# The output projection of 16 tiles in pairs, by seven products of quarters under one bounded scale

## The chip, the cores and the metric

The kernel runs on one core of one Trainium2 chip. Its time is the device time of one execution in microseconds (us); for a kernel the median of its runs is given. One execution was also recorded by the hardware profiler. The engines are called PE (TensorE matmul), PEld (its weight loads), DVE (VectorE), ACT (ScalarE), POOL (GpSimd) and SP (SyncE, which only issues DMAs here).

## What is computed

One step of a network layer for two groups of tokens: 2048 sample tokens and 128 prompt tokens, 2176 rows of 1024 float32 values. Three branches mix the tokens, each branch is projected to 1024 columns and gated, the three are added (`merged`), and one output projection, a residual add and a normalisation end it. The part that matters here:

```python
    br = jnp.stack([o_a, o_b, o_c], axis=2)
    pb = jnp.einsum('btnw,nwd->btnd', br, w_branch)
    gt = jax.nn.sigmoid(gates.reshape(B, T, N_BRANCH, D_MODEL))
    merged = jnp.einsum('btnd,btnd->btd', gt, pb)
    return jnp.einsum('btd,de->bte', merged, w_out), s_f, s_b
...
        out, _, _ = mixer(xn, *lp(l), state_delta[:, l, 0], state_delta[:, l, 1], (rows, GRID_W))
        h = h + gate[:, None, :] * out
    y_sample = rmsnorm(h, final_g)
```

`merged` is (2176, 1024), `w_out` is (1024, 1024). For the sample group the gate is one row of 1024 values, for the prompt group another.

## The kernel before

Rows are counted in 17 tiles of 128 (`P`): tiles 0 to 15 are the sample tokens, tile 16 the prompt. The 1024 columns of the model are eight blocks (`KT`) of 128. Every float32 operand of a large product is split into two float16 halves: it is multiplied by a power of two `s` found from its sum of squares (`scales`: a square with accumulated sum on ACT, a one-column matmul with ones on PE for the sum over the partitions, three integer steps on DVE), `hi` is the float16 of that (ACT), `lo` the float16 of the rest (DVE). A product then takes three matmuls per block of 128 in the contraction: hi·hi, hi·lo, lo·hi (`gemm_T`, `gemm_N`). A result is multiplied by the inverse scales where it leaves PSUM.

Three merges come one after the other, `merge(1)`, `merge(2)` and `merge(0)`, each adding one branch to `merged`, which is kept transposed in DRAM (`mD`: block of columns, 128, tokens). In a merge, for each column block `db` and each stretch of 512 tokens (the last stretch, the prompt, has 128): 24 matmuls of the gate from the normalised input `xh`, `xl` (which stays in SBUF all the time), a sigmoid on ACT, 12 matmuls of the branch projection from `o16` (in the pool `big`), the product on DVE (L1708), the addition to the old row on POOL (L1709), which SP has loaded (L1687); after each half of the tokens POOL's queue writes the row back (L1716). In the last merge `HALVES` is turned round, so tokens 1024 to 2175 come first in each block and tokens 0 to 1023 last. During it `out_w` loads and splits one block of `w_out` per `db`, and the gate rows are made. During the second merge the scan of the DeltaNet branch still runs, with its own loads in SP's queue.

After the last merge the output: tile 16, then tiles 8 to 15, then 0 to 7. For each tile `out_prep` loads the tile's eight blocks from `mD` (L1767), squares them, finds the scale and makes the halves (L1777 to L1780); this runs five tiles ahead of the products, for the first five already in the last merge. Then two products of 512 columns over eight blocks (48 matmuls a tile), the gate times the inverse scales on the way out of PSUM (L1841), the residual add on POOL (L1842), the square, the root and the scaling by `final_g` (L1860 to L1862) and the store. The last tile is cut into 512, 384 and 128 columns so that little is left after its last product.

The order on each engine is fixed when the program is built: a scheduler places the instructions by estimated durations and by priorities (`tc.high_priority`), and each engine then runs its list in order. SP's list holds nearly all loads and the stores of the results, so a load whose buffer is not free yet holds back all loads behind it. Buffers rotate within a pool by tag (`bufs`); memory of a closed pool is used again by later pools once its last readers are done. PSUM has eight banks: three in `ps_mm`, three in `ps_d`, two in `ps_x`.

Of the kernel before, what the change touches and what calls it, by code (L numbers as in the profile page):

```python
# [188 lines left out]
def hybrid_flow_kernel(ctx: ExitStack, tc: tile.TileContext, x_prompt, x_sample, state_delta, c, c_ctx, w_ada,  # L189
# [50 lines left out]
    def mm(out, l, r, start=True, stop=True):  # L240
        newest[0] = PE.matmul(out, l, r, start=start, stop=stop)  # L241
# [16 lines left out]
    def scales(ss, pl, tag, sb16=None):  # L258

        ps = bank(ps_x, [P, 1])  # L260
        mm(ps, ones16, widened(ss, pl, tag) if sb16 is None else sb16)
        t = sb(pl, [P, 4], tag)
        h = t[:, 3:4].bitcast(I32)
        V.tensor_scalar(h, ps.bitcast(I32), 24, None, ALU.logical_shift_right)
        V.tensor_scalar(t[:, 1:2].bitcast(I32), h, -8388608.0, 204.0 * 8388608, ALU.mult, ALU.add)
        V.tensor_scalar(t[:, 2:3].bitcast(I32), h, 8388608.0, 50.0 * 8388608, ALU.mult, ALU.add)
        return t[:, 1:2], t[:, 2:3]
# [20 lines left out]
    def converting(w, st, nkt, cols=P, hi=None, lo=None, tag="w", bufs=5):  # L288
# [9 lines left out]
        ss = sb(wp, [P, 1], "wss", bufs=4)  # L298
# [45 lines left out]
    for i, (n_, g) in enumerate(_blocks()):  # L344
        wlist.append((w_blk[i], KT, "z" if n_ == C_ZA else "v" if n_ == C_V else "w", 4))
        if n_ >= C_G:
            wlist.append((w_brb[(n_ - C_G) // D, g], 4, "b", 2))
# [4 lines left out]
    def read_next(p_=None):  # L352
# [4 lines left out]
        elif len(wread) < min(len(wdone) - len(wsteps) + 2, len(wlist)):  # L357
            src, nkt, tag, bufs = wlist[len(wread)]
            wread.append(read_w(src, nkt))

    def begin():
# [7 lines left out]
        wsteps.append(converting(wdone[i], wread[i], wlist[i][1], tag=wlist[i][2], bufs=wlist[i][3]))  # L369
# [1288 lines left out]
    def branch_scale(n, cols):  # L1658
        ss = sb(ep, [P, 1], "bss2")
        V.tensor_reduce(ss, oss[n][:, 0:cols], AX.X, ALU.add)  # L1660
        return scales(ss, ep, "bsc")
# [10 lines left out]
    def merge(n, first, inv, each=None, halves=HALVES, mid=None, then=None):  # L1672

        steps, sinv = iter(()), None
        for db in range(KT):
# [8 lines left out]
            for h0, hn, tbs in halves:  # L1684
# [5 lines left out]
                for t0, tn in tbs:  # L1690
                    if first and db == 0:
# [14 lines left out]
                    else:  # L1706
                        with tc.high_priority():
                            V.scalar_tensor_tensor(sg, ps, binv[:, 1:2], sg, ALU.mult, ALU.mult)  # L1708
                        G.tensor_tensor(mr, mr, sg, ALU.add)  # L1709
                    pace.tick(tn * MT)  # L1710
# [5 lines left out]
                (SY if first else G).dma_start(mD[db][:, h0:h0 + hn], mrow)  # L1716
# [29 lines left out]
    def finish_delta(db):  # L1746
        if db == KT - 1:
# [9 lines left out]
    winv = sb(orp, [P, KT], "winv8")  # L1757

    def out_w(i):
        w = load_w(w_outb[i], KT, hi=whi[:, :, i * P:(i + 1) * P], lo=wlo[:, :, i * P:(i + 1) * P])  # L1760
        V.tensor_mul(winv[:, i:i + 1], w.inv, sx)

    turn = []

    def out_prep(t, pl, tag, hl=None):
        mt = sb(pl, [P, KT, P], tag, bufs=2)
        SY.dma_start(mt, mD[:, :, t * P:(t + 1) * P].rearrange("k p t -> p k t"))  # L1767
        if hl is None:
            mh = sb(orp, [P, KT, P], "mh", F16, bufs=3)
            ml = sb(orp, [P, KT, P], "ml", F16, bufs=3)  # L1770
        else:
            mh = sb(wp, [P, KT, P], "whi", F16, bufs=4)
            ml = sb(wp, [P, KT, P], "wlo", F16, bufs=4)
        ss = sb(orp, [P, 1], "mss", bufs=2)
        with tc.high_priority():
            with tc.issue_after(turn[0].ins) if len(turn) > 2 else ExitStack():
                A.activation(ml, mt, AF.Square, accum_out=ss)  # L1777
            s, inv = scales(ss, orp, "msc")
            turn.append(A.activation(mh, mt, AF.Copy, scale=s))  # L1779
            V.scalar_tensor_tensor(ml, mt, s, mh, ALU.mult, ALU.subtract)  # L1780
        inv8 = sb(orp, [P, KT], "inv8", bufs=6)
        V.tensor_scalar(inv8, winv, inv, None, ALU.mult)
        return mh, ml, inv8

    pre, gp = [], []

    def half_gate(i):
        t = sb(ep, [P, 512], "st", bufs=3)
        SY.dma_start(t, gateD[1:2, i * 512:(i + 1) * 512].to_broadcast([P, 512]))
        gp.append(t)  # L1790

    def ahead_out(h0):
        if h0:
            for i, t in enumerate(order[:5]):
                pre.append(out_prep(t, *((wp, "wst") if i % 3 else (big, "mrow")), None if i < 3 else wp))
            for i in range(2):
                half_gate(i)
                scale_gate(gp[i], gp[i], pre[0][2][:, 4 * i:4 * i + 4])
# [6 lines left out]
    order = [16] + list(range(8, 16)) + list(range(8))  # L1805
    def tail(db):
        out_w(db)
# [8 lines left out]
    op = pool(ctx, "op", 2)  # L1816
    gb = sb(op, [P, D], "gb", bufs=1)
    SY.dma_start(gb, gateD[0:1, :].to_broadcast([P, D]))
    fg = sb(op, [P, D], "fg", bufs=1)
    SY.dma_start(fg, final_g[None, :].to_broadcast([P, D]))  # L1820

    part = sb(op, [P, 3], "part", bufs=1)
    for i_, t in enumerate(order):
        mh, ml, inv8 = pre[i_]
        end = i_ == 16
        xr = sb(op, [P, D], "xr")
        SY.dma_start(xr, xrows(t * P, P))
        hh = sb(op, [P, D], "hh")
        ss2 = sb(op, [P, 1], "hss")
        if i_:  # L1830
            gt = sb(op, [P, D], "gt")
            scale_gate(gt, gb, inv8)
        if end:
            hf = sb(op, [P, D], "gt")
        for i, (c0, c1) in enumerate([(0, 512), (512, 896), (896, D)] if end else [(0, 512), (512, D)]):
            cs = slice(c0, c1)
            ps = bank(ps_mm, [P, c1 - c0])
            gemm_N(ps, mh, ml, wo, c0, c1 - c0)
            dst, gc = (hh[:, cs], gt[:, cs]) if i_ else (gp[i], gp[i])
            with tc.high_priority():  # L1840
                V.tensor_tensor(dst, ps, gc, ALU.mult)  # L1841
            (V if end else G).tensor_tensor(hh[:, cs], dst, xr[:, cs], ALU.add)  # L1842
            if end:
                A.activation(xr[:, cs], hh[:, cs], AF.Square, accum_out=part[:, i:i + 1])
                (V if i == 2 else G).tensor_tensor(hf[:, cs], hh[:, cs], fg[:, cs], ALU.mult)
                if i:
                    V.scalar_tensor_tensor(part[:, i:i + 1], part[:, i:i + 1], 1.0 / D, part[:, i - 1:i], ALU.mult, ALU.add)
                else:
                    V.tensor_scalar(part[:, 0:1], part[:, 0:1], 1.0 / D, EPS, ALU.mult, ALU.add)
        if i_ < 12:  # L1850
            pre.append(out_prep(order[i_ + 5], op, "mt"))
        out = y_sample[0, t * P:(t + 1) * P] if t < 16 else y_prompt[0]
        if end:
            G.tensor_tensor(ss2, part[:, 2:3], mhalf, ALU.pow)
            V.tensor_scalar(hf[:, 0:640], hf[:, 0:640], ss2, None, ALU.mult)
            A.activation(hf[:, 640:D], hf[:, 640:D], AF.Copy, scale=ss2)
            SY.dma_start(out[:, 0:640], hf[:, 0:640])
            A.dma_start(out[:, 640:D], hf[:, 640:D])
        else:
            A.activation(xr, hh, AF.Square, accum_out=ss2)  # L1860
            rsqrt(ss2, ss2, 1.0 / D, 1)
            V.scalar_tensor_tensor(hh, hh, ss2, fg, ALU.mult, ALU.mult)  # L1862
            SY.dma_start(out, hh)
# [28 lines left out]
```

## Time and profile before

| | |
|---|---|
| time, median of 3 runs | 2180.16 us (2175.74 to 2181.94) |
| the profiled execution's own time | 2174.15 us |
| its span, first to last instruction | 2172.3 us |
| mean granted TensorE clock | 0.995 |
| moved by DMA | 371.90 MB, mean 171 GB/s |

In the views below, a group's line gives source line, engine, operation, output and inputs by the program's names, shapes, count, busy time, mean ns of one, and the idle time of the engine ahead of it with what ended it. The span in 40 equal slices, each digit the busy share in tenths:

```profile
PE   8999999999899999999899999899999999999998
DVE  6657754389779798466655556765563544233454
ACT  5554744466556664455544446655553422222332
POOL 0321332233434422444222223354532222212543
PEclk9999999999999999999999999999999999999999
DMA  9525632276776743444755556776664533334542
```

The last merge fills slices 32 to 36, the output the last three and a bit. Line numbers in the profile are those of the kernel before; a line can be that of a helper (L241 is every matmul of `mm`, L278 every weight load).

### The profile page before, as it was taken

Reading aid. Unit: us, or ns where it says so; the run is one execution under the profiler, and the core shown is the slowest. Engines: PE = TensorE matmul, PEld = TensorE weight load, DVE = VectorE, ACT = ScalarE, POOL = GpSimd, SP = SyncE. Lnnn points to the kernel's source line nnn. Section 1 sums busy time; section 2 is a strip of 40 time slices with the busy share of each in tenths; the row PEclk is TensorE's granted clock in tenths of the full one; section 3 lists DMA queues with packets and bytes.
Section 4 is the critical chain, followed back from the end, with each engine's and each line's share of the span. In section 5 each row is a group of like instructions: output and inputs, shape, how many; then the busy total and the mean of one; then the engine's idle time right before and its main releaser. Section 6 shows DMA issues by size and latency. Waiting matters only on the chain. (4 is left out here: it accounts for less than half of the span.)

```text
span 2172.3 us, 42588 instructions
## 1 busy us (share of the span) xinstructions
PE 2102.9 (97%) x16249; PEld 1204.3 (55%) x16249; DVE 1314.2 (60%) x3049; ACT 1037.8 (48%) x2388; POOL 704.2 (32%) x869
## 2 busy tenths in 40 slices
PE   8999999999899999999899999899999999999998
PEld 4455444465455677787455556556555544444444
DVE  6657754389779798466655556765563544233454
ACT  5554744466556664455544446655553422222332
POOL 0321332233434422444222223354532222212543
PEclk9999999999999999999999999999999999999999
DMA  9525632276776743444755556776664533334542
GB/s 353 218 72 201 250 119 83 93 234 218 235 235 218 227 141 91 138 142 119 234 163 160 164 168 188 239 216 198 195 199 139 177 129 122 114 102 132 170 149 103
DMA packets 228748, 371.90 MB, mean 171 GB/s; under 512 B 38952, under 2 KB 125504, under 8 KB 226240
## 3 DMA queue, kind: packets, MB, share of 16 engines
q1 hardware_dynamic: 176032, 274.20, 40.3%
q0 software_dynamic: 12688, 51.27, 6.5%
q10 hardware_dynamic: 39824, 43.72, 6.0%
q8 instruction: 127, 2.08, 0.4%
q14 instruction: 77, 0.63, 0.1%
HBM read 241.48 MB, written 127.62 MB: 170 GB/s over the span
## 5 line engine op out<-in xcount | busy, mean ns | idle before, releaser
L241 PE MATMUL b<-xh,whi 128*128 128x512 f16 (+1 forms) x1920 | 649.7, 347 | 2.8 <-DVE sg L1436 2.5
L241 PE MATMUL b<-xl,whi 128*128 128x512 f16 (+1 forms) x1920 | 650.0, 347 | 0.0
L241 PE MATMUL b<-xh,wlo 128*128 128x512 f16 (+1 forms) x1920 | 649.0, 347 | 0.0
L241 PEld LDWEIGHTS <-whi 128*128 128x128 f16 x3904 | 355.7, 98 | 327.9 <-issue 8.6
L241 PEld LDWEIGHTS <-wlo 128*128 128x128 f16 x1952 | 191.0, 98 | 176.9 <-issue 1.4
L241 PE MATMUL b<-big,bhi 128*128 128x512 f16 (+1 forms) x960 | 250.8, 347 | 4.2 <-ACT big L1669 2.6
L1709 POOL TENSOR_TENSOR mrow<-mrow,sg 128x512 f32<-128x512 f32 (+1 forms) x80 | 93.4, 1169 | 283.2 <-DVE sg L1708 173.0
L241 PE MATMUL b<-big,blo 128*128 128x512 f16 (+1 forms) x480 | 162.9, 347 | 0.2 <-DVE blo L312 0.2
L1699 ACT ACTIVATE sg<-b,winv 128x512 f32<-128x512 f32 (+1 forms) x120 | 74.1, 618 | 132.6 <-PE b L241 132.1
L241 PEld LDWEIGHTS <-xh 128*128 128x128 f16 x1496 | 118.3, 99 | 30.0 <-issue 1.8
L1708 DVE SCALAR_TENSOR_TENSOR sg<-b,binv,sg 128x512 f32<-128x512 f32 (+1 forms) x80 | 53.4, 668 | 129.0 <-PE b L241 120.8
L241 PEld LDWEIGHTS <-bhi 128*128 128x128 f16 x960 | 86.4, 98 | 79.8 <-issue 4.4
L936 POOL TENSOR_TENSOR cy<-cy,raw 128x545 f32<-128x545 f32 (+1 forms) x48 | 64.4, 1366 | 180.6 <-ACT raw L935 180.6
L255 DVE CAST wscb<-wss 128x1 bf16<-128x1 f32 x89 | 13.7, 154 | 138.2 <-ACT wlo L299 57.6
L241 PE MATMUL b<-whi,xh 128*128 128x128 f16 x544 | 94.5, 221 | 1.8 <-DVE yT L1622 1.0
L1170 POOL COPY T<-ES 32x256 f16<-32x256 f16 x68 | 29.2, 430 | 201.2 <-DMA ES<-ei 178.2
L241 PE MATMUL b<-wlo,xh 128*128 128x128 f16 x544 | 94.4, 221 | 0.0
L241 PE MATMUL b<-whi,xl 128*128 128x128 f16 x544 | 94.4, 221 | 0.0
L241 PE MATMUL b<-wohi,mh 128*128 128x512 f16 (+2 forms) x248 | 91.9, 372 | 0.2 <-ACT mh L1779 0.2
L241 PE MATMUL b<-wohi,ml 128*128 128x512 f16 (+2 forms) x248 | 91.7, 372 | 0.3 <-DVE ml L1780 0.3
L241 PE MATMUL b<-wolo,mh 128*128 128x512 f16 (+2 forms) x248 | 91.9, 372 | 0.0
L312 DVE SCALAR_TENSOR_TENSOR wlo<-wst,wsc,whi 128x1024 f16<-128x1024 f32 x52 | 71.2, 1370 | 33.1 <-ACT whi L311 32.9
(481 smaller groups left out, 4241.3 us busy)
## 6 DMA issues: line engine op xcount, KB each, us to landing
wst<-in_w_blk_dram SPq DMA_DIRECT2D x58, 512.0 KB, 5.7
qkv<-cy POOLq DMA_DIRECT2D x12, 1089.0 KB, 5.3
st<-br SPq DMA_DIRECT2D x48, 256.0 KB, 3.8
mrow<-mrg SPq DMA_DIRECT2D x18, 512.0 KB, 3.8
mrow<-mrg SPq DMA_DIRECT2D x16, 576.0 KB, 4.4
mrg<-mrow POOLq DMA_DIRECT2D x16, 576.0 KB, 3.9
dc<-dec SPq DMA_DIRECT2D x17, 512.0 KB, 4.4
kq<-qkv SPq DMA_DIRECT2D x34, 256.0 KB, 4.9
```

The source lines that it names most:

```text
L241: newest[0] = PE.matmul(out, l, r, start=start, stop=stop)
L255: V.tensor_copy(sb16, ss)
L312: w.low = V.scalar_tensor_tensor(w.lo, st, s, w.hi, ALU.mult, ALU.subtract)
L936: G.tensor_tensor(y[:, c0:c1], y[:, c0:c1], raw[:, 1 + c0:1 + c1], ALU.mult)
L1170: G.tensor_copy(T16[rows(a0, b), :, :, b], ES[0:32, :, 2 * a0 + b, :, wT])
L1699: A.activation(sg, ps, AF.Sigmoid, scale=gw.inv)
L1708: V.scalar_tensor_tensor(sg, ps, binv[:, 1:2], sg, ALU.mult, ALU.mult)
L1709: G.tensor_tensor(mr, mr, sg, ALU.add)
```

## The change

The rows of `merged` are taken in pairs of tiles (256 tokens), and a pair's product with `w_out` is a product of two matrices of two by two quarters: 128 tokens by 512 columns on one side, 512 by 512 on the other. Strassen's scheme (in Winograd's form) makes it with seven products of quarters in place of eight and with sums of quarters on both sides. Tile 16 is still done by itself.

- *One scale.* The pairs' operands share one power of two, from a bound instead of their own squares: for each branch its sum of squares times the largest sum of squares of a block of `w_branch`, the three added, times three. The squares of `w_branch` are kept in `bsums` where the blocks are converted anyway; those of branch 0 are loaded and squared for it in the second merge (`finish_delta`).
- *w_out.* `out_w` runs four times with two blocks each; on top of the halves of the eight blocks it makes the four sums of quarters (POOL), their halves, and writes these to DRAM (`tD`).
- *The rows.* In the last merge, where `db` is 4 to 7, the row of block `db - 4` is loaded too (`m4`), and `quarters` makes the four sums (three additions on DVE, one on POOL), the halves of all seven operands, and writes them to DRAM (`paD`). The rows of these blocks are no longer written to `mD` but for the prompt's.
- *The output.* Each pair's seven operands are loaded from `paD` (14 KB a partition, two buffers in the pool `op`, a third where `out_w` and `quarters` had their desk), the summed quarters of `w_out` from `tD` into the place of `xl`, rows of x and results lie in the place of `xh`. `two_tiles` does the seven products in three banks, some of them adding to a bank that has been read already.

The core of the diff:

```diff
+    def out_w(j):
+        for st, i in zip(sts, (j, j + 4)):
+            SY.dma_start(st, w_outb[i].rearrange("p (k c) -> p k c", c=P))
...
+        for i in range(2):
+            halves(whi[:, :, cols_[i]], wlo[:, :, cols_[i]], sts[i], s)
+        t1, t2 = [tmp[:, i * 512:(i + 1) * 512].rearrange("p (k c) -> p k c", k=4) for i in range(2)]
+        b11, b21, b12, b22 = [st[:, q] for st in sts for q in q4]
+        for q, out, x, y in ((0, t1, b12, b11), (1, t2, b22, t1), (2, t1, b22, b12), (3, t2, b21, t2)):
+            G.tensor_tensor(out, x, y, ALU.subtract)
+            slot = slots[:, (4 * j + q) % 3]
+            halves(slot[:, 0], slot[:, 1], out, s)
+            G.dma_start(tD[q, :, j, :], slot.rearrange("p l k c -> p (l k c)"))
+
+    def quarters(k, t0, m4, mr):
...
+        V.tensor_tensor(S[:, :, 0], x4[:, :, 1], x8[:, :, 1], ALU.add)
+        G.tensor_tensor(S[:, :, 2], x4[:, :, 0], x4[:, :, 1], ALU.subtract)
+        V.tensor_tensor(S[:, :, 1], S[:, :, 0], x4[:, :, 0], ALU.subtract)
+        V.tensor_tensor(S[:, :, 3], x8[:, :, 0], S[:, :, 1], ALU.subtract)
+        halves(T7[:, :, 0, 0], T7[:, :, 1, 0], x4[:, :, 0], ms_s)
+        halves(T7[:, :, 0, 1:3], T7[:, :, 1, 1:3], x8, ms_s)
+        halves(T7[:, :, 0, 3:7], T7[:, :, 1, 3:7], S, ms_s)
+        G.dma_start(paD[t0 // 256:t0 // 256 + 2, k].rearrange("a p x -> p a x"), T7.rearrange("p a l n c -> p a (l n c)"))
...
     def finish_delta(db):
+        st = sb(ep, [P, 512], "st", bufs=3)
+        SY.dma_start(st, w_brb[0, db])
+        A.activation(st, st, AF.Square, accum_out=bsums[:, 3 + db:4 + db])
...
                 for t0, tn in tbs:
+                    m4 = None
+                    if n == 0 and db > 3 and tn == 512:
+                        m4 = sb(ep, [P, tn], "st", bufs=3)
+                        SY.dma_start(m4, mD[db - 4][:, t0:t0 + tn])
...
                         G.tensor_tensor(mr, mr, sg, ALU.add)
+                    if m4 is not None:
+                        quarters(db - 4, t0, m4, mr)
...
-                (SY if first else G).dma_start(mD[db][:, h0:h0 + hn], mrow)
+                if n or db < 4:
+                    (SY if first else G).dma_start(mD[db][:, h0:h0 + hn], mrow)
+                elif h0:
+                    G.dma_start(mD[db][:, NS:NTOK], mrow[:, NS - h0:NTOK - h0])
...
+    room = xh.rearrange("p k t -> p (k t)").bitcast(F32)
+    tw = xl.rearrange("p k t -> p (k t)")[:, 0:16 * D].rearrange("p (q j l k c) -> p q j l k c", q=4, j=4, l=2, k=4)
+    firsts = [8, 10, 12, 14, 0, 2, 4, 6]
...
+    def next_pair():
+        i = len(ready)
+        if i < len(firsts):
+            ready.append(operands(op, 2) if i % 3 else operands(orp, 1))
+            SY.dma_start(ready[i].rearrange("p k l n c -> p k (l n c)"), paD[firsts[i] // 2].rearrange("k p x -> p k x"))
...
+    next_pair()
+    for q in (1, 2, 0, 3):
+        SY.dma_start(tw[:, q].rearrange("p j l k c -> p j (l k c)"), tD[q])
...
+    def product(ps, pa, n_, w, fresh):
+        hi, lo = [pa[:, :, l, n_] for l in range(2)]
+        for k in range(4):
+            mm(ps, hi[:, k, :], w(0, k), fresh and k == 0, False, not fresh)
+            mm(ps, hi[:, k, :], w(1, k), False, False, not fresh)
+            mm(ps, lo[:, k, :], w(0, k), False, k == 3, not fresh)
...
+    def two_tiles(t, pa, xr, hh, end):
...
+        product(a, pa, 0, quarter(0, 0), True)
+        with tc.high_priority():
+            A.copy(p1, a)
+        product(Y, pa, 4, summed(1), True)
+        total(u2, Y, p1)
+        product(a, pa, 1, quarter(4, 0), False)
+        with tc.high_priority():
+            V.tensor_tensor(hh[0][:, left], a, gb[:, left], ALU.mult)
+        (V if end else G).tensor_tensor(hh[0][:, left], hh[0][:, left], xr[0][:, left], ALU.add)
+        product(Y, pa, 5, summed(2), False)
+        total(u3, Y, p1)
+        product(X, pa, 3, summed(0), True)
+        total(hh[1][:, right], X, u3)
+        gated(1, right)
+        product(Y, pa, 2, summed(3), False)
+        total(hh[1][:, left], Y, p1)
+        gated(1, left)
+        if not end:
+            product(X, pa, 6, quarter(4, 512), False)
+            total(hh[0][:, right], X, u2)
+            gated(0, right)
+            for j in (1, 0):
+                rows_done(t + j, hh[j], xr[j])
+            return
...
+    xr, hh = two_rows(16, 1)
+    ahead_rows = two_rows(firsts[0], 2)
+    next_pair()
+    next_pair()
+    one_tile(16, pre[0], xr[0], hh[0])
+    for i, t in enumerate(firsts):
+        rows_ = ahead_rows
+        if i < 7:
+            ahead_rows = two_rows(firsts[i + 1], 2)
+        two_tiles(t, ready[i], *rows_, i == 7)
+        next_pair()
```

A pair is named by its first tile: pair 8 is tiles 8 and 9, pair 10 is tiles 10 and 11. In the built program the scheduler sets three products of pair 10 ahead of pair 8, whose operands lie in the third buffer, and from there on mixes the products of neighbouring pairs.

More of the change, by code (lines that the diff above doesn't have):

```diff
@@ L1783, in out_prep @@
[L1783 to L1798, printed above, removed]
+            halves(hl[0], hl[1], mt, s)
@@ L1800, in scale_gate @@
+        return hl, inv
     def scale_gate(out, src, inv):
@@ L1817, in hybrid_flow_kernel @@
     gb = sb(op, [P, D], "gb", bufs=1)
+    fg = sb(op, [P, D], "fg", bufs=1)
+    part = sb(op, [P, 3], "part", bufs=1)
     SY.dma_start(gb, gateD[0:1, :].to_broadcast([P, D]))
[L1819 to L1863 removed]
```

160 lines of the change are left out of this document (132 added, 28 removed).

## The prediction

> **What bounds the kernel now.** I read the page's busy times first, then the stages by windows, then the end of the chain of waits, because the change lies in the last two stages.
>
> ```profile
> PE 2102.9 (97%) x16249; PEld 1204.3 (55%) x16249; DVE 1314.2 (60%) x3049; ACT 1037.8 (48%) x2388; POOL 704.2 (32%) x869
> ```
>
> ```profile
> 1700.00:1988.00 288.00, 287.76 (x1594) 139.87 (x1593) 107.23 (x263) 84.20 (x136) 60.63 (x62) 1.00 0.38 124
> 1988.00:2165.00 177.00, 176.67 (x855) 81.30 (x853) 88.72 (x167) 52.97 (x79) 83.75 (x69) 1.00 0.45 149
> 2165.00:2173.00 8.00, 0.00 (x0) 0.00 (x0) 2.03 (x6) 1.47 (x5) 1.43 (x2) 0.80 0.18 67
> ```
>
> The columns are the stretch, its length, busy time (and count) of PE, weight loads, DVE, ACT and POOL, the granted clock, the DMA share and GB/s. The last merge (1700 to 1988) and the output (1988 to 2165) leave PE idle for 0.2 and 0.3 us; everything else has half of the time free, DMA too. So matmul count times pitch is the time there.
>
> ```profile
> 1989.05 175.92 PE b L241 x851
> 2164.99 0.30 DVE hh L1841
> 2165.32 0.72 DVE hh L1842
> 2166.06 0.41 ACT xr L1844 x2
> 2166.50 0.17 DVE part L1847
> 2166.77 0.59 POOLq L1888
> 2167.38 0.61 ACT gt L1856
> ```
>
> The chain that ended last is one run of 851 matmuls and then a tail of 7.3 us (2164.99 to the span's 2172.3).
>
> **The change, part by part.**
>
> *Fewer products.* Before, 17 tiles cost 48 matmuls of 512 columns each, 816 in all. After, eight pairs cost seven products of 12 (84) and tile 16 its 48: 720. The pitch comes from the starts of 18 adjoining matmuls, 17 gaps:
>
> ```profile
> 1963.28 0.38 PE L241 MATMUL b<-xh,whi 128*128 128x512 f16 x1
> 1966.94 0.38 PE L241 MATMUL b<-xh,wlo 128*128 128x512 f16 x1
> ```
>
> 3.66/17 = 0.2153 us. 96 fewer are 20.7 us, all on the path. The 15 one-column scale products that disappear too change it by under 1 us; left out.
>
> *What the pairs wait for.* This decides. Before, five tiles were converted ahead, so PE went from merge to output without a gap. In the built order of the changed kernel PE does tile 16 (48 matmuls), then three products of pair 10 (36), then pair 8. Their operands come by DMA, and SyncE issues in this order: rows of x and the four summed quarters of w_out (into xh and xl, so each waits for the last gate matmuls that read those rows), then gb, fg and pair 10's operands (into memory of the branch operands, so they wait for the merge's last matmul, M), pair 12's, rows of x, tile 16's result, and only then pair 8's. Sizes from the shapes, 128 partitions each: a quarter 4096 float16 = 1.05 MB, x rows or gb or fg 0.52, a pair 7168 float16 = 1.84. POOL's queue adds the last two operand writes, 0.92 each. From the first quarter to pair 10: 4 x 1.05 + 5 x 0.52 (three rows of x, gb, fg) + 1.84 + 2 x 0.92 = 10.5 MB. On to pair 8: 1.84 + 2 x 0.52 + 1.84 = 4.7 MB.
>
> The first quarter may go when xl's fourth row has been read, about 11 matmuls into the last gate product of 24, which is followed by 12: M - 25 x 0.2153 = M - 5.4. How fast the queue then drains, by rows:
>
> ```profile
> 20.00:30.00 10.00, 8.37 (x44) 3.97 (x45) 5.38 (x13) 4.92 (x9) 0.00 (x0) 1.00 1.03 413
> 30.00:40.00 10.00, 7.01 (x42) 3.68 (x41) 9.40 (x32) 4.88 (x9) 0.00 (x0) 1.00 1.03 408
> ...
> q1 hardware_dynamic: 176032, 274.20, 40.3%
> q0 software_dynamic: 12688, 51.27, 6.5%
> ...
> skn<-kv SPq DMA_DIRECT2D x34, 256.0 KB, 2.8
> ```
>
> With all engines busy the start of the kernel moved 410 GB/s, in rows of 4 KB and more. Over the run, bytes by share of the span give 274.2/(0.403 x 2172) = 313 GB/s for SyncE's queue, with many short packets, and 363 for POOL's with 4 KB ones. The runs here are 3.5 and 8 KB long, so near the top: I take 390, bounds 313 and 410. A lone 256 KB load lands in 2.8 us where 410 GB/s would need 0.6: 2.2 us fixed, which I split 1.4 ahead and 0.8 behind (an estimate).
>
> Pair 10 lands at M - 5.4 + 1.4 + 10.5/0.39 + 0.8 = M + 23.7 and pair 8 at 4.7/0.39 = 12.1 later, M + 35.8. PE wants pair 10 at M + 48 x 0.2153 = M + 10.3 and, unhindered, pair 8 at M + 18.1. So two waits, 13.4 us and then the rest, put the remaining 636 matmuls 17.7 us late. At 410: 15.8; at 313: 27.3. Behind pair 8 a pair takes 84 x 0.2153 = 18.1 us and moves 1.84 + 4 x 0.52 = 3.9 MB, 217 GB/s, with two pairs buffered: no further wait.
>
> *PE after a wait.* The start shows what idle time does to the clock:
>
> ```profile
> 39.91 1.01 PE L182 MATMUL b<-xh,zhi 128*128 128x512 f16 x2 [2.41 <-ACT xh L182]
> ...
> 40.00:42.00 2.00, 2.00 (x5) 0.61 (x5) 2.00 (x4) 1.92 (x4) 0.00 (x0) 0.50 1.16 485
> 42.00:44.00 2.00, 2.00 (x8) 0.81 (x7) 2.00 (x4) 2.00 (x4) 0.00 (x0) 0.67 0.98 418
> ```
>
> After 2.41 us of idling the clock was 0.50 for 2 us and 0.67 on the mean of the next 2, so half speed for about 3.3 us: 1.7 us lost. After the first wait this lies inside the second (36 products take 9.4 us, pair 8 is then still 2.7 us off). After the second it is on the path: +1.7, or 0 if that wait is too short. The Trainium skill, "TensorE: Matmul & The Clock Gate", Part 1, says that the clock halves after an idle window of about 3.4 us and needs as long to come back, the window running free; by it the second wait of 2.7 us may or may not cost the 1.7 us, while the row says that 2.4 us of idling can suffice.
>
> *Operands in the last merge.* Sixteen times (blocks of 512, db 4 to 7): three additions of 256 on DVE and one on POOL, halves of 256, 512 and 1024 on ACT and DVE, one DMA write from POOL. By-form rows of the last merge and of the output:
>
> ```profile
> L1708 DVE SCALAR_TENSOR_TENSOR sg<-b,binv,sg 128x512 f32<-128x512 f32 x34 | 25.5, 750 | 95.4 <-PE b L241 90.2 <-issue 4.7 <-ACT sg L1699 0.4
> L312 DVE SCALAR_TENSOR_TENSOR wolo<-wst,wsc,wohi 128x1024 f16<-128x1024 f32 x8 | 10.2, 1281 | 3.5 <-ACT wohi L311 3.5
> L311 ACT ACTIVATE wohi<-wst,wsc 128x1024 f16<-128x1024 f32 x8 | 9.2, 1146 | 14.6 <-DVE wsc L265 14.6
> L1709 POOL TENSOR_TENSOR mrow<-mrow,sg 128x512 f32<-128x512 f32 x34 | 44.6, 1311 | 195.3 <-DVE sg L1708 105.2 <-DVE wsc L264 90.2
> L1716 POOL DMA_DIRECT2D mrg<-mrow x17 | 9.7, 571 | 6.7 <-POOL mrow L1709 4.8 <-issue 1.9
> ```
>
> DVE: 0.75 for the eviction, about 1.2 for the sums (0.75 x 256/512 each), 2.3 for the halves (1792 elements at 1.28 per 1024): 4.3 of a block's 36 x 0.2153 = 7.75 us. POOL: 1.31 + 0.65 + 0.57 = 2.5. The latency matters more: eviction 0.85, POOL's add to 2.2, two sums to 3.0, half of mr to 3.8, third sum to 4.2, ACT's 1024 to 5.4, DVE's 1024 to 6.7, POOL's DMA and next difference to 7.9, just before the next add at 8.5. DVE's next eviction queues behind that, but PE needs the bank only a block later (three banks, two per block), so it is covered by some 7 us; without that cover a slip costs its own length. I take +1, bounds 0 and +10 (0.6 per block). w_out takes four doubled steps in place of eight and eight more sums; they stand in the merge's first half, which has more room: 0.
>
> *The bound.* Eight squares of w_branch move into the second merge. Their loads stand in SyncE's queue ahead of the scan's next operands, and only three buffers serve them, so later loads wait for ACT's earlier squares. The place in the trace of before:
>
> ```profile
> 1397.13 1.31 SPq L1153 DMA_DIRECT2D ES<-ei  x3
> 1399.42 0.34 SPq L1254 DMA_DIRECT2D sv<-kv  x1
> ...
> 1401.37 0.63 ACT L299 ACTIVATE blo<-wst 128x512 f16<-128x512 f32 x1 [1.83 <-DMA wst<-in_w_brb_dram]
> 1401.91 0.19 ACT L299 ACTIVATION_READ_ACCUMULATOR blo<-wst 128x1 f32 x1
> ```
>
> A square and its read take 0.8 us, eight 6.6, issues 8 x 0.33 = 2.6; ACT is idle about as long there. The scan's step slips by some 3 us, once; PE, in order, may wait for it. Bounds 0 and +5: I take +2.
>
> *Tail.* ACT's square (1.05) and DVE's scaling (1.28) of the partner row now stand among the last tile's steps in the built order, about half of each on the path: +1.3, bounds 0 and +2.5. The new additions and gates of the output use engines that are half idle: 0.
>
> **Sum**, against the profiled span of 2172.3: -20.7 + 17.7 + 1.7 + 1 + 2 + 1.3 = +3.0, 2175.3. The shown median 2180.16 lies 7.9 above the span, so I add 3.0 to it: 2183.
>
> **Rivals.**
>
> *The operands come in time* (the change gives its 20.7 us). Speaks for it: DMA is under half busy on the mean of both stages. Against: the queue is in order and 10.5 MB cannot pass in the 15.7 us from M - 5.4 to M + 10.3; that takes 670 GB/s, and no window shows more than 485. Time: -20.7 + 1 + 1.3 = -18.4, 2162. Chance 0.06.
>
> *The backlog drains at the start's rate*, 410, with no slow clock and no lost step: -20.7 + 15.8 + 1 = -3.9, 2176; if the two POOL writes (4.5 us) also fall outside the queue, -8.4, 2172. For it: the kernel's first 40 us. Chance 0.20.
>
> *Slower: the backlog drains slowly.* One mechanism: the loads of pairs 10 and 8, at 313 to 363 GB/s instead of 390; it decides below about 363, where the waits alone pass 20.5 us and eat all that the products save. For it: SyncE's average of 313, and reads that share the engines with POOL's writes. At 363 the waits are 20.5 us, at 313 27.3: with the other terms +5.8 to +12.6, 2186 to 2193. Chance 0.24. The Trainium skill, "DMA: Bandwidth & Descriptors", Where 436 GB/s comes from, speaks for this: between HBM and SBUF a core's share of the HBM, about 358 GB/s, binds before the fabric's 435. By that the time would be 2187; the trace's windows of 408 to 413 do not agree with it for one core alone.
>
> *Slower: the last merge is overrun*: DVE's chain passes 7.75 us a block and evictions come a bank late; +10 or more, 2193 to 2200. For it: the 0.6 us margin above. Against: DVE's 4.3 of 7.75 us. Chance 0.08.
>
> **How the numbers follow.** The forecast (gain and waits cancel, 2179 to 2187) has 0.42. I call 0.3% (6.5 us) the border of what can be told from no change. Faster: the first rival, under half of the second, a little of the forecast: 0.2. Slower: the last rival, most of the third and the upper edge of the forecast: 0.34. Same: 0.46. The range takes the second rival's lower end and the third's upper one with the merge's bound: 2168 to 2198; the forecast's own is 2176 to 2190.
>
> **What would show it.** PE's count in the output falls by 96 of 512 columns. PE has a gap of about 13 us some 10 us after the merge ends, released by a pair's DMA, a second of some 3 us about 9 us later, a granted clock of 0.5 behind each, and DMA windows at 390 GB/s or more across both. The last merge keeps its 288 us within 1, and the scan's wait near 1400 grows by 2. I am wrong if PE runs through the start of the output, if the gaps stand elsewhere, or if the last merge grows by many us.

## The result, and the profile after

The changed kernel takes 2193.38 us (median of 15 runs, 2185.07 to 2205.11), the kernel before 2177.54 (15 runs, 2171.23 to 2186.21): ratio 1.0071, 95% interval 1.0053 to 1.0088. By the ratio that is 15.5 us more; the forecast was 3.0 more. The profiled execution has a span of 2183.3 and took 2185.07, the shortest of its 15, so its excess over the profile of before, 11.0 us, is a low sample.

The same stages by windows, the columns as in the prediction (last merge, output, tail):

```profile
1700.00:1998.00 298.00, 292.40 (x1608) 141.61 (x1607) 176.60 (x362) 123.79 (x191) 112.56 (x118) 1.00 0.53 180
1998.00:2174.00 176.00, 159.18 (x734) 71.48 (x732) 68.03 (x90) 24.30 (x42) 91.43 (x80) 0.95 0.55 211
2174.00:2184.00 10.00, 0.00 (x0) 0.00 (x0) 3.29 (x9) 2.56 (x7) 2.06 (x3) 0.55 0.27 106
```

The output lasts 176 us where it had 177, though 96 products of 512 are gone (734 recorded matmuls for 855): PE is idle for 17 us of it. The last merge, in which PE stood for 0.2 us, now loses 5.6 and ends 10.5 us later than before (at 1998.27, where the tile 16 matmuls start, against 1987.73). The view of PE's waits from 1690 on names both (us in total, times, longest):

```profile
PE b L241 <- DMA pa<-pa: 14.4, 2, 14.1
PE b L241 <- DVE sg L1720: 5.5, 5, 1.8
PE b L241 <- DVE st L1967: 1.6, 1, 1.6
PE b L241 <- DVE xh L2003: 0.6, 1, 0.6
```

**The start of the output** looks as predicted. PE's timeline, the last matmul of tile 16, the first of pair 10 and of pair 8, and the windows of the wait:

```profile
2008.52 0.38 PE L241 MATMUL b<-wohi,wlo 128*128 128x512 f16 x1
2023.03 0.58 PE L241 MATMUL b<-wohi,pa 128*128 128x512 f16 x1 [14.13 <-DMA pa<-pa]
...
2028.10 5.41 PE L241 MATMUL b<-xl,pa 128*128 128x512 f16 x24
2033.79 0.39 PE L241 MATMUL b<-wohi,pa 128*128 128x512 f16 x1 [0.28 <-DMA pa<-pa]
```

```profile
2000.00:2010.00 10.00, 8.89 (x42) 3.81 (x39) 4.97 (x7) 1.87 (x2) 5.25 (x6) 1.00 1.01 390
2010.00:2020.00 10.00, 0.00 (x0) 0.00 (x0) 1.89 (x2) 1.15 (x2) 3.50 (x3) 0.56 1.01 419
2020.00:2030.00 10.00, 6.97 (x21) 2.68 (x22) 0.00 (x0) 0.00 (x0) 0.00 (x0) 0.59 1.03 410
```

With M = 1998.27, pair 10 arrives at M + 24.8 (forecast 23.7), the wait is 14.1 us, DMA is full at 390 to 419 GB/s in these windows, and the clock stands at half. The first twelve matmuls take 2028.10 - 2023.03 = 5.07 us where 12 x 0.2153 = 2.58 us would do: 2.5 us are lost. Pair 8 is then late by only 0.28, and behind it the clock is full.

**The tail.** The end of the chain of waits:

```profile
2172.34 0.57 DVE xh L2003
2172.91 0.02 issue
2172.93 1.26 DVE xh L2004
...
2174.90 0.64 ACT xh L1919
...
2176.20 0.56 POOL hss L251
2176.76 0.02 issue
2176.78 1.28 DVE xh L1921
```

The partner row's square (L1919) and scaling (L1921) stand between the last tile's own steps, as predicted. L2004, an addition of 384, takes 1.26 us; before, the same step (L1842) took 0.56. An addition of POOL for the partner row runs beside it, from 2172.51 to 2173.78.

**Where the time went, in all profiles.** For each trace I took every group of ACT and DVE instructions that has the same count in it and in the trace of before, and the median of how much later its members start, in windows; PE's last matmul of the merge (it starts at 1998.05 in the changed kernel, at 1987.11 in the one before: 10.9 us later), PE's end and the span give the rest. The table has, against the profile of before, the us gained or lost up to 1390 (A), from there to the end of the second merge near 1650 (B), to the last matmul of the last merge (C), to PE's end (D), and in the tail (E). The runs e1 to e12 are those of the next section.

| profile | A | B | C | D | E | sum |
|---|---|---|---|---|---|---|
| e8, before again | 3.1 | 0.8 | -0.4 | -0.2 | 0.0 | 3.3 |
| after | 0.9 | 3.6 | 6.5 | -2.1 | 2.1 | 10.9 |
| e1 three plain tiles | 3.4 | 7.3 | 13.5 | -11.4 | 2.6 | 15.4 |
| e2 no squares | -2.1 | 3.2 | 7.6 | -1.3 | 1.8 | 9.2 |
| e3 sums on DVE | 2.0 | 6.3 | 9.9 | -1.0 | 2.1 | 19.2 |
| e4 pair first | 3.4 | 6.1 | 10.5 | 0.9 | 2.2 | 23.2 |
| e5 six banks | 4.0 | 6.7 | 2.5 | 0.9 | 1.8 | 15.8 |
| e6 squares, no loads | 9.7 | 1.6 | 8.0 | -2.0 | 1.8 | 19.1 |
| e10 e5 + early squares | 4.3 | -2.2 | 1.7 | 1.4 | 2.2 | 7.4 |
| e7 all mended | 6.1 | 0.9 | 0.7 | -15.7 | 3.6 | -4.3 |
| e9 | 13.7 | 2.6 | -0.1 | -10.4 | 1.1 | 6.9 |
| e11 | 7.3 | -1.1 | 0.7 | -15.1 | 1.1 | -7.1 |
| e12 | 10.6 | 3.5 | 0.1 | -13.8 | 1.1 | 1.5 |

Column A is mostly chance: up to 1390 us the built order of e6 is that of the changed kernel, and they have 9.7 and 0.9. The other columns go with the edits. Where a kernel keeps the changed kernel's own code for a stage, B is 3.6 to 7.3 (five profiles), C 6.5 to 10.5 (after, e2, e4, e6), D -2.1 to -1.0 (after, e2, e3, e6) and E 1.8 to 2.6.

### The profile page after: what moved, and what is told of

It is laid out like the page before. It is cut to its first block, busy times and chain, and to the rows that moved or that the text cites. A ratio compares the mean times of both kernels' runs of the same rounds, so it can differ in the third digit from the quotient of the medians.

```text
span 2183.3 us, 42589 instructions
## 1 busy us (share of the span) xinstructions
PE 2086.8 (96%) x16122; PEld 1193.9 (55%) x16122; DVE 1357.1 (62%) x3070; ACT 1056.4 (48%) x2428; POOL 765.5 (35%) x939
## 5 line engine op out<-in xcount | busy, mean ns | idle before, releaser
L241 PEld LDWEIGHTS <-whi 128*128 128x128 f16 x3872 | 353.0, 98 | 329.9 <-issue 14.5
L1721 POOL TENSOR_TENSOR mrow<-mrow,sg 128x512 f32<-128x512 f32 (+1 forms) x80 | 99.2, 1242 | 153.0 <-DVE sg L1720 119.3
L241 PEld LDWEIGHTS <-pa 128*128 128x128 f16 x684 | 66.9, 99 | 98.3 <-issue 20.7
L305 ACT ACTIVATE wlo<-wst 128x1024 f16<-128x1024 f32 x52 | 55.0, 1058 | 70.1 <-DMA wst<-in_w_blk_dram 65.2
L241 PE MATMUL b<-xl,pa 128*128 128x512 f16 x384 | 86.7, 379 | 1.6 <-DVE st L1967 1.6
L241 PEld LDWEIGHTS <-xl 128*128 128x128 f16 x816 | 74.6, 99 | 13.4
```

The lines of the kernel that those rows point to most:

```text
L241: newest[0] = PE.matmul(out, l, r, start=start, stop=stop, skip_group_check=reopened)
L305: w.squared = A.activation(w.lo, st, AF.Square, accum_out=ss)
```

## The experiments

**e8: how far one kernel moves.** The kernel before, profiled again, without an edit.

> The kernel before once more, for a second profile of it. Every theory: ratio 1. It tells how far the steps of one and the same kernel move between two profiles: under 1 us between 1400 and the end if the lags read so far are the change's own, up to 3 us if the scan's stage plays by chance.

One run, 2177.46 us, span 2175.7: 3.1 us later by 1390, within 0.8 in each stage behind it. That is a single pair of profiles, and C differs by 4 us between kernels with the same code in the last merge; so I read a value of B to E as an edit's only where it lies outside the ranges just given, and no single value of A.

**e1: three plain tiles.** Theory: the output's start waits for bytes.

```diff
-    firsts = [8, 10, 12, 14, 0, 2, 4, 6]
+    firsts = [10, 12, 14, 0, 2, 4, 6]
...
+            pre.extend([plain(8), plain(9)])
...
+    for j in range(2):
+        one_tile(8 + j, pre[1 + j], xr8[j], hh8[j])
```

> Tiles 8 and 9 are computed the old way (48 products each, halves made in the last 15 us of the merge with the bounded scale, no squares), tile 16 as now, then seven pairs. Theory (the start of the output waits for bytes that no order of issue can bring earlier): PE has 144 matmuls of its own, 31 us, while pair 10 lands about 25 us after the merge's last matmul; the 14.1 us gap, the 0.3 us gap and the half clock behind them (about 2.6 us) go, 12 matmuls more cost 2.6 us: 14.4 us less than the changed kernel's profile, span near 2169, ratio to the kernel before 0.998 to 1.001. Rival (the loads are slow because PE idles or because the pairs' memory is handed over late): the gap moves behind tile 9 and keeps over 5 us; span 2175 or more.

2187.2 us, ratio 1.0043 (1.0029 to 1.0057): 6 us won, not 14.4. No wait for a pair is left, and D falls to -11.4, but C doubles to 13.5. Behind the merge PE waits for tile 16's halves (1.6 and 1.9 us). In the merge it stands for 9.6 us, but at places between 1749 and 1962, before the halves of tiles 8 and 9 are made; the longest stop, 3.15 us up to 1857.10, was followed by 5.3 us at half clock, some 2.5 us more. Why the merge of this kernel loses more than the changed kernel's is not shown. The rival's gap behind tile 9 did not come. So the start of the output was understood, the merge was not.

**e4: the order of the loads.** Three rows of x and final_g behind pair 10.

```diff
+    with tc.issue_after(loads[1].ins):
+        xr, hh = two_rows(16, 1)
+        ahead_rows = two_rows(firsts[0], 2)
+        SY.dma_start(fg, final_g[None, :].to_broadcast([P, D]))
```

> Three rows of x and the row of final_g are issued behind pair 10's load instead of ahead of it (1.6 MB); same matmuls in the same order. Theory (bytes in an in-order queue): pair 10 lands 3.8 us earlier, about 21 us behind the merge's last matmul, but pair 8 still has the same bytes ahead of it and lands where it did, 35 us behind; the first wait falls to 10.3 us, the second grows from 0.3 to about 4, the sum and the time stay within 1 us. Rival (the first pair alone decides): 3.8 us less in all.

2196.35 us, ratio 1.0082 (1.0064 to 1.01). PE's timeline of this kernel:

```profile
2026.80 0.58 PE L241 MATMUL b<-wohi,pa 128*128 128x512 f16 x1 [8.87 <-DMA pa<-pa]
2031.87 5.39 PE L241 MATMUL b<-xl,pa 128*128 128x512 f16 x24
2043.03 0.61 PE L241 MATMUL b<-wohi,pa 128*128 128x512 f16 x1 [5.76 <-DMA pa<-pa]
```

8.87 + 5.76 = 14.6 us against 14.13 + 0.28 = 14.4: the first wait shrinks and the second grows by as much. It is bytes in an in-order queue. The sum of the waits stayed, as expected, but D did not stay within 1 us: it is 0.9 for -2.1. The clock stood at half behind both waits, the first time up to 2031.87 (5.07 us), the second time from 2043.03 to 2048.12 (5.09 us, granted 0.50), so the 2.5 us were lost twice; in the changed kernel they were lost once.

**e2 and e6: the squares.** e2 drops the eight loads and squares, e6 the loads alone. The diff is e6's; in e2 nothing stands in place of the two lines.

```diff
-        SY.dma_start(st, w_brb[0, db])
-        A.activation(st, st, AF.Square, accum_out=bsums[:, 3 + db:4 + db])
+        A.activation(st, xh[:, db, 0:512], AF.Square, accum_out=bsums[:, 3 + db:4 + db])
...
+    V.tensor_copy(bsums[:, 3:11], bsums[:, 11:19])
```

> Leaves out the eight loads and squares of the first branch's weights in the second merge (the bound takes the second branch's sums in their place); all else as changed. Theory (their loads block SyncE's queue from 1401.7 to 1406.6, the load of the scan's norm rows and a weight load come late behind them): the steps between 1400 and 1440 keep the times of the kernel before within 1 us where they were 8 us late, and 3.8 us of the total come back: ratio to the kernel before 1.0050 to 1.0060, span near 2179.5. Rival (ACT's 6.6 us of squares are what delays the scan, not the queue): the same gain, so this run does not tell the two apart. Rival (the scan's place shifts from run to run): no change of the lag near 1420 beyond 2 us.

> The eight squares stay in the second merge on ACT, but of columns of x that lie in SBUF already, so SyncE's queue has none of their eight loads; the bound takes the second branch's sums. Theory (the loads block SyncE's queue in order): the steps near 1430 are at most 2 us later than without squares, time as without the squares, about 2186, ratio 1.003 to 1.0045. Rival (the 6.6 us of squares on ACT delay the scan): the lag near 1430 stays at 6 to 9 us, time near 2193.

e2: 2186.07 us, ratio 1.0038 (1.0023 to 1.0054). e6: 2191.83, ratio 1.0056 (1.004 to 1.0071). Both missed their ratios: with e2 more came back than the 3.8 us expected, and e6 lies near its rival's 2193. The intervals of e6 overlap those of e2 and of the changed kernel, so the times do not tell loads from squares. The traces do, for the step that was expected to move. From 1390 to 1430 e6 fell back by 1.2 to 3.6 us (its lags jump there, so it depends on the window) and e2 by 3.5, the five kernels with the loads by 6.0 to 7.1. At the end of the second merge the difference is less sharp. The seven profiles without these loads in the second merge have B from -2.2 to 3.5, mean 1.2; the five with them 3.6 to 7.3, mean 6.0; but e2 with 3.2 and the changed kernel with 3.6 are almost alike. SyncE's queue in the changed kernel:

```profile
1399.44 0.84 SPq L1765 DMA_DIRECT2D st<-in_w_brb_dram  x2
1401.03 0.33 SPq L1261 DMA_DIRECT2D sv<-kv  x1
1401.73 4.87 SPq L1765 DMA_DIRECT2D st<-in_w_brb_dram  x3
1406.72 1.32 SPq L1373 DMA_DIRECT2D br<-o  x1
...
1409.37 0.33 SPq L1358 DMA_DIRECT2D of<-of  x1
```

and of the kernel before, at the same place:

```profile
1399.42 0.34 SPq L1254 DMA_DIRECT2D sv<-kv  x1
1403.55 0.38 SPq L1366 DMA_DIRECT2D br<-o  x1
1404.32 0.33 SPq L1351 DMA_DIRECT2D of<-of  x1
```

From 1401.73 to 1406.60 the queue issues three loads, each waiting for one of three buffers that an earlier square must leave; the scan's `of` goes out 5.0 us later than before, the rest of its loads behind it. In e2 it goes out at 1404.08. The squares themselves on ACT cost nothing that shows near 1430; there it is the queue in order. The expectation that without them the steps near 1430 keep their time within 1 us failed: they were 3.5 us late, and near 1490 6.7 at most, where the changed kernel has 6.3; half of that was caught up by 1650. The kernel before itself moved by 2.0 there (e8).

**e3 and e5: the last merge.** Two ideas on why evictions come late. One place, in the changed kernel, DVE and then PE:

```profile
1774.82 0.87 DVE L466 SCALAR_TENSOR_TENSOR sg<-wst,scT,sg 128x256 f32<-128x256 f32 x2
1775.61 1.41 DVE L1793 SCALAR_TENSOR_TENSOR pa<-sums,wsc,pa 128x512 f16<-128x512 f32 x2
1777.33 0.83 DVE L1805 TENSOR_TENSOR oss2b<-oss 128x1 bf16<-128x1 f32 x1 [0.32 <-ACT wolo L1803]
1778.14 0.16 DVE L255 CAST wscb<-wss 128x1 bf16<-128x1 f32 x1
1778.21 0.74 DVE L1720 SCALAR_TENSOR_TENSOR sg<-b,binv,sg 128x512 f32<-128x512 f32 x1
```

```profile
1779.01 0.38 PE L241 MATMUL b<-xh,whi 128*128 128x512 f16 x1 [1.51 <-DVE sg L1720]
```

The eviction could go when the block's last matmul had ended (1775.5) and ACT's sigmoid (1776.27), but it stands in DVE's queue behind w_out's halves and behind L1805, which waits for w_out's squares on ACT. It comes 2 us late, and all three banks are taken: PE stops. A second thing is seen beside POOL, again on DVE:

```profile
1739.29 3.94 DVE L1793 SCALAR_TENSOR_TENSOR pa<-sums,wsc,pa 128x512 f16<-128x512 f32 x2 [1.60 <-ACT pa L1792]
```

The same two steps take 3.94 us here and 1.41 above. Here two additions of POOL keep their time (1.28 us each, at 1739.51 and 1740.73) and DVE is held up. Above, POOL adds as well, from 1773.78 to 1778.14: 4.36 us for one addition, while DVE keeps its time. So one of the two engines is held up, not always the same. The Trainium skill, "GPSIMD Engine Reference", 1. Specifications, says that GpSimd shares its SBUF interface with VectorE and that the two contend when a DVE instruction has two SBUF inputs; these halves have two, and the trace agrees. Is that what costs? e3 takes POOL's additions away:

```diff
-            G.tensor_tensor(out, x, y, ALU.subtract)
+            V.tensor_tensor(out, x, y, ALU.subtract)
```

> The sixteen subtractions of w_out's quarters go from POOL to DVE (512 columns each), all else as changed. Theory (POOL's adds of two SBUF operands hold up DVE's operations that read two SBUF operands: a pair of halves took 3.9 us beside them and 1.4 without): the evictions that came late near 1743 and 1779 come in time, the last merge loses 1 to 2 us of idle time where the changed kernel has 5.5, although DVE has 11 us more to do; last merge 3 us shorter. Rival (DVE's queue is simply too full, or waits in order for ACT's squares): the idle time stays at 5 us or grows to 7.

2192.76 us, ratio 1.0067 (1.005 to 1.0083); PE stands for 7.7 us in the last merge, as the rival had it, and C is 9.9, inside the 6.5 to 10.5 of the kernels with these sums on POOL. The contention is real, but taking it away from these steps did not bring the evictions in time; what it costs by itself is not shown, as DVE had the sixteen subtractions to do as well. e5 leaves all work as it is and gives PE more banks:

```diff
-                    ps = bank(ps_mm, [P, tn])
+                    ps = bank(ps_mm if n else ps_d, [P, tn])
                     gemm_T(ps, bw, 0, o16[:, 0, :, t0:t0 + tn], o16[:, 1, :, t0:t0 + tn], nkt=4)
```

> One edit to the changed kernel: in the last merge the branch product goes to the three PSUM banks that the scan has left, so that the gate's and the branch's products have three banks each in place of three together. Theory (PE stands in the last merge because an eviction on DVE is queued behind w_out's or the quarters' steps that wait for ACT, POOL or a landing, and three banks cover only about one block of that): the idle of 5.5 to 8 us in the last merge falls under 1 us, the merge's lag against the kernel before from 6 to 10 us to 1, time 6 to 8 us under the changed kernel's 2193.4, ratio 1.0035 to 1.0045. Rival (DVE and ACT have too much work for the merge, a matter of throughput): the waits come later but stay, over 4 us of idle.

2189.89 us, ratio 1.0051 (1.0031 to 1.0071). C falls to 2.5 and no wait for an eviction is left up to 2000 (the same view as above):

```profile
PE b L241 <- DVE blo L318: 1.2, 1, 1.2
PE b L241 <- DVE mscb L255: 1.0, 1, 1.0
```

So it was latency and not throughput. The time missed its expectation all the same (1.0035 to 1.0045; 3.5 us won for 6 to 8). What PE gains it partly hands back: it now reaches the output ahead of ACT, waits 5.8 us for tile 16's halves and then 8.4 for pair 10, in sum what it waited before, since the bytes start no earlier.

**e10 and e7: do the causes add up?** e10 is e5 with the squares moved to the second branch's gating, before 1069 us. e7 adds three plain tiles (tile 16 too under the bounded scale) and, in the last pair, the partner row's products first.

```diff
+        if n == 1 and ti in (1, 3):
+            k = 2 * g + ti // 2
+            st = sb(ep, [P, 512], "st", bufs=3)
+            SY.dma_start(st, w_brb[0, k])
+            A.activation(st, st, AF.Square, accum_out=bsums[:, 3 + k:4 + k])
...
+            pre.extend([plain(t) for t in (16, 8, 9)])
```

> The changed kernel with six banks in the last merge and the squares moved to the gating of the second branch; eight pairs, one plain tile and the tail as changed. Theory (the start of the output costs what it did, whatever the merge does): the wait for pair 10 plus the half clock behind it are again 14 to 17 us, so the time lies 12 to 15 us over the mended kernel with three plain tiles: ratio to the kernel before 1.003 to 1.0045. Rival (three plain tiles gain only 6 us, as they did alone): ratio 1.0 to 1.001.

> Tiles 16, 8 and 9 plain with the bounded scale, seven pairs, six banks in the last merge, the squares moved to the gating of the second branch (before 1069 us), and in the last pair the partner row's products ahead of the first row's left half. Theory (the change's losses are these four and they add up): against the kernel before 84 matmuls fewer, 18.1 us, and no wait at the start of the output, 0 to 3 us lost elsewhere: 2160 to 2165, ratio 0.992 to 0.9945. Rival (moved work only shows up in another place, as with the three plain tiles alone): the merge is again 8 us or more late, 2172 or more, ratio 0.997 to 1.0.

e10: 2188.3 us, ratio 1.0042 (1.0029 to 1.0055). e7: 2175.31, ratio 0.9975 (0.996 to 0.9989), 0.25% faster than the kernel before, with an interval clear of 1. Between e10 and e7 lie 0.67% or 14.5 us, what e1 promised and did not give while the merge was overrun. e7's windows of merge, output and tail:

```profile
1700.00:1995.00 295.00, 294.39 (x1620) 142.70 (x1619) 179.37 (x356) 119.50 (x189) 113.43 (x123) 1.00 0.53 175
1995.00:2157.00 162.00, 158.76 (x746) 72.30 (x743) 68.71 (x94) 27.68 (x46) 82.33 (x75) 1.00 0.60 230
2157.00:2168.00 11.00, 0.00 (x0) 0.00 (x0) 4.73 (x9) 2.67 (x7) 3.79 (x5) 0.60 0.25 96
```

B and C are 0.9 and 0.7, the output 15.7 us shorter. The ratio of 0.992 to 0.9945 was still missed: the tail grew to 11 us instead of shrinking, one eviction waited 2.0 us behind final_g's landing, and A took 6.1. The five kernels with the squares before 1069 us have A from 4.3 to 13.7, mean 8.4, the seven other changed kernels 3.0 on the mean (-2.1 to 9.7); so the squares' new place may cost again what it saves. That was not tried apart.

**e9, e11, e12: the tail and final_g.** All three put the partner row's gating in the last pair on DVE. e9 also loads the gate row and final_g ahead of w_out's sums; e11 and e12 leave the loads as in e7 and issue the closing steps of tiles 16, 8 and 9 behind their evictions. In e11 those steps overwrite a row of x that pair 10 still needs, so a part of the samples' result differs; e12 writes elsewhere and also fixes the order by `issue_after`, which e11 does not have. In the diff the first lines are in all three, the last two are e12's.

```diff
-            G.tensor_tensor(hh[j][:, cs], hh[j][:, cs], gb[:, cs], ALU.mult)
+            for other, op_ in ((gb, ALU.mult), (xr[j], ALU.add)):
+                (V if end else G).tensor_tensor(hh[j][:, cs], hh[j][:, cs], other[:, cs], op_)
...
+    with tc.issue_after(ev.ins):
+        rows_done(16, hh[0], hh[1])
```

> The mended kernel (three plain tiles, seven pairs, six banks, early squares, partner row first) with two more edits: the gate row and final_g are loaded ahead of w_out's sums, and in the last pair the partner row's gating (four operations of 512) goes from POOL to DVE. Theory (in the mended kernel one eviction waits 2.0 us because DVE stands behind final_g's landing; and the tail of 11.0 us holds two DVE operations of 1.63 and 1.24 us that take 0.56 and 0.29 without POOL's adds beside them): both go, tail 8 to 9 us, 3 to 4 us less than the mended kernel: ratio 0.9955 to 0.9965. Rival (the quarters' sums, now 5 us later, make the first pair wait, or DVE's four operations of 0.69 lie on the path themselves): no gain, 0.997 to 0.999.

> The mended kernel of the seventh run (its order of loads, w_out's sums first), with the partner row's gating of the last pair on DVE, and the closing steps of tiles 16, 8 and 9 issued behind the evictions of all three, so that no eviction stands behind final_g's landing. Theory (both edits take what they take in the profile: the tail went from 11.0 to 8.5 us in the run before, the wait of 2.0 us behind final_g goes or halves, and pair 10 is not late): 3 to 4 us less than the seventh run, ratio 0.9955 to 0.9965. Rival (the run-to-run spread hides them, or the closing steps pile up in front of the pairs' own evictions): 0.997 to 0.9985.

> As the run before, but the squares of tile 16's closing step go to a row that is free, not over the row of x that pair 10 still needs. Theory: the same time as the run before within its interval, ratio 0.994 to 0.997, no eviction behind final_g's landing, tail 8.5 us. Rival (the run before was quick only because of the overwritten row): 0.9975, as the seventh run.

Ratios 0.9972 (0.9959 to 0.9985), 0.9951 (0.9933 to 0.9968) and 0.9974 (0.9954 to 0.9994). The tail shortens in all three, E from 3.6 to 1.1. In e9 the rival came true: w_out's sums, now behind, let PE wait 4.4 us for pair 10 (D -10.4). e12's ratio is the one that its rival named, and it is no faster than e7 within the intervals. Its D lost 1.9 us: PE stands for 3.1 us at 2159, where two closing steps (L1921, 2.28 and 1.29 us) stand in DVE's queue ahead of an eviction. So these edits are not shown to pay, and whether e11 was really quicker stays open.

## Why the prediction was right and where it was wrong

The time lies in the range, 10 us above the forecast and outside the forecast's own range (2176 to 2190). That the range holds it is partly luck: its upper end was built from a slow drain of the queue, which did not happen, and from the merge's bound. The likeliest case, no measurable change, did not come. The rival with 0.08, an overrun last merge, came by its effect, evictions a bank late, but not where it put the cause: it had the quarters' chain pass 7.75 us a block, and most of the waits lie at w_out's steps. Its time, 2193, was reached only together with another term that was too small.

- *Fewer products and the operands' arrival*: right. Pair 8 started 35.5 us after M (2033.79), forecast 35.8. Pair 10 landed 1.1 us later than worked out, at 390 to 419 GB/s: from 1993.2 to 2022.2 the engines moved 395 GB/s, 11.5 MB for the 10.5 counted, among them a third operand write of POOL (issued at 2008.31) that the sum did not have. The sentence drawn from the Trainium skill, "DMA: Bandwidth & Descriptors", Where 436 GB/s comes from, with 358 GB/s for reads from HBM, does not hold here: this core alone moved 410 to 419. The rival of a slow drain fell with it.
- *The clock after the wait*: half right. Behind the first wait the lost time lies inside the second one, as said; it was 2.5 us for 1.7, and the second wait shrank from 2.7 to 0.28 us. The +1.7 of the sum stood behind the second wait, and there nothing was lost: from 2030 on the granted clock was 1.00. The prediction had named 0 for that case. In the last pair PE then waited 1.6 and 0.6 us for evictions (L1967 and L2003 in the view of waits), which no term had; so the output as a whole, forecast -20.7 + 17.7 + 1.7 = -1.3 and measured -2.1, came out right in part by luck. The Trainium skill, "TensorE: Matmul & The Clock Gate", Part 1, has at least one busy window of about 3.4 us, the window running free, until full speed returns; here it was 5.07 us.
- *Operands in the last merge*: here the prediction failed. It took +1 for the quarters and 0 for w_out, "they stand in the merge's first half, which has more room"; measured 6.5, and 6.5 to 10.5 over the four profiles that keep its code. Of the 5.5 us of waits in the changed kernel two, 3.3 us, lie at w_out's steps, one, 1.0 us at 1847, behind w_out's last halves and the quarters' first, and two, 1.2 us, at the quarters', which the +1 had about right. The room that was counted was DVE's busy share; what mattered was what stands in DVE's queue ahead of an eviction and waits for ACT (L1805 above), with three banks to cover it. e5 shows it: the same work with six banks, 2.5.
- *The bound's squares*: mechanism right, size wrong. Named were the loads ahead of the scan's operands and buffers that later loads wait for; priced were one slip of 3 us and +2, at most +5. Measured 3.6 in the profile, 6.0 on the mean of five, 4.8 more than the mean without the loads, with the reserve on B made above. The queue stood 4.87 us at a stretch, longer than the 3 counted, and everything of the scan behind it came late.
- *Tail*: +1.3 within 0 to 2.5; measured 2.1. Not foreseen was POOL's gating of the partner row, beside which L2004 took 1.26 us for 0.56.
- *The sum*: on the mean of the profiles that keep the code D is -1.6, C 8.2, B 6.0 less the 1.2 of the kernels without the loads, and E 2.1: 13.5 us, near the 15.5 of the ratio. The forecast had 3 for C and B, and got 13: by the table these are the 10 us that were missing. Taking both causes away gave back less: e10, with six banks and without the loads in the second merge, has a ratio of 1.0042 for 1.0071, 6.3 us. Pair 10's bytes come no earlier there, so PE waits for tile 16's halves and for the pairs again (5.8 and 10.3 us, D 1.4), and A is 4.3.

Not settled are the spread ahead of 1390 us, which the change does not touch, and how much of B is the loads'.

## What to carry to other kernels

Where a step is said to be hidden, ask what stands in the same queue behind its waits, and how many banks or buffers cover that latency; an engine's busy share answers another question. Here loads that share a small ring of buffers held back every later load of their in-order queue, for 4.87 us; what is urgent should not stand behind such loads. Operands that can only be loaded into memory that the stage before still uses need work of the old kind in front of them: three plain tiles covered 10 MB here, but won 6 us while the stage before had three banks and 14.5 once it had six. And where bytes set the end of two waits, making the first one shorter did not help: two waits of 8.87 and 5.76 us cost the half clock twice.

## What the runs showed that was not expected

- The same instructions in the same order, up to 1390 us, came 0.9 us later than before in one profile and 9.7 in another. Part of it goes with the clock; the stretch from 900 to 1069 in the changed kernel and in e6, granted 0.98 and 0.96:

```profile
900.00:1069.00 169.00, 156.87 (x2027) 119.19 (x2024) 106.38 (x275) 88.37 (x217) 61.19 (x101) 0.98 0.50 152
```

```profile
900.00:1069.00 169.00, 159.03 (x2102) 123.90 (x2100) 106.36 (x277) 87.70 (x216) 63.33 (x103) 0.96 0.50 147
```

- After 14.1 us of idling PE ran 5.07 us at half clock; after 2.41 us, in the kernel before, 3.3. In e3 a stop of 2.89 us in the last merge was enough (half clock from 1748.91 to 1751.86), in e12 a stop of 3.08 us (up to 2159.08) was not: the granted clock stayed at 1.00. So the length of a stop alone does not decide.
- POOL suffers from the contention as well: one of its additions of 512, otherwise 1.28 us, took 4.36 beside DVE's halves and gate steps, which kept their time:

```profile
1773.78 4.36 POOL L1721 TENSOR_TENSOR mrow<-mrow,sg 128x512 f32<-128x512 f32 x1 [3.20 <-DVE sg L1720]
```
